# A streaming encoder step: 44 of 48 merge-gate blocks by Strassen's seven products

## The chip, the cores and the metric

One core of one Trainium2 chip runs the kernel in one launch. The metric is the device time of that core in microseconds, smaller is better; an execution is timed from outside, and one further execution is profiled instruction by instruction.

## The reference, cut to what matters

One layer for 640 tokens (512 of a prompt, 8 streams of 16): a pre-norm, one projection to the heads of three attention branches and to three merge gates of the model width, the attentions, and the merge. The change concerns the gates.

```python
D_MODEL = 2048
x2 = rms_norm(x, g_pre)                      # 640 tokens
mg_sb, mg_bd, mg_mm = split(x2 @ w_in)[-3:]  # 3 gates of 2048 columns each
merged = (sigmoid(mg_sb) * ((o_sb * silu(g_sb)) @ w_up_sb)
          + sigmoid(mg_bd) * ((o_bd * silu(g_bd)) @ w_up_band)
          + sigmoid(mg_mm) * ((o_mm * silu(g_mm)) @ w_up_mem))
y = x + rms_norm(merged @ w_out, g_post)
```

## The kernel before, in words

All operands are float32, and every matmul is done as three float32r matmuls. `split` (line 91) cuts an operand into a high part, which ACT writes (line 92), and the residual, which DVE computes (line 93); the products high by high, high by low and low by high are added up in PSUM. Transposed x stands in SBUF as `xh` and `xl` (128 partitions, 16 blocks of the model width, 640 tokens).

A projection block, `proj` (line 129), yields 128 output columns for all 640 tokens. It loads the block's weights in slabs of 8 x 128 rows (`load_w`, line 95: `wr` has three buffers, `wh` and `wl` two each), splits them, and for each of 16 k issues three matmuls for each half of 320 tokens (line 139), 96 in all, into two PSUM banks. The program order is: the prologue (pre-norm by `norm_x`, memory keys and values); 16 heads, each with four projections and its attention, its gated output `sg` written to DRAM (`spill`, line 516); then the merge; then the output projection.

The merge runs over 48 gate blocks (`gate`, line 587) and 48 up-projection blocks (`up`, line 601), 16 of each for each of the three branches. `up(i)` follows four blocks behind `gate(i)`, the sigmoid of a gate stays in SBUF in between. At the first block of a branch `up` loads the branch's heads back from DRAM (`load_o`, line 593: `or` has two buffers, `oh` and `ol` six) and splits them. DVE multiplies the block by its sigmoid (lines 611, 613), and from the second branch on POOL adds it to `merged` (line 614).

```python
for i in range(3 * KB + AHEAD):
    if i < 3 * KB:
        gate(i)
    if i >= AHEAD:
        up(i - AHEAD)
gh, gl = xh, xl
```

A scheduler puts the instructions of each engine in order, from this program text and its own model of the engines; it lets later blocks fill the gaps of earlier ones, so the first gate blocks stand between the instructions of the last head. Each engine, and each DMA queue, then works strictly in its order. A pool of tiles that is opened after another was closed reuses its space, and the first instruction that writes a tile there waits for the last ones that used what lies under it.

Of the kernel before, what the change touches and what calls it, by code (L numbers as in the profile page):

```python
# [41 lines left out]
def stream_step_kernel(  # L42
# [19 lines left out]
    xpool = ctx.enter_context(tc.tile_pool(name="xpool", bufs=1, side="right"))  # L62
# [4 lines left out]
    # 1 where a new key of the same stream lies strictly before the query, and the complement;  # L67
    # rows in the order of the sample columns, keys in that of the streams
# [3 lines left out]
    xh = xpool.tile([P, KB, NT], F32R, name="xh")  # L72
    xl = xpool.tile([P, KB, NT], F32R, name="xl")
# [3 lines left out]
    osg_d = [dpool.tile([P, NT], F32, name=f"osg_d{i}") for i in range(16)]  # L77

    # Sample row or column 32 j + 16 a + i is token i of stream 4 a + j.
    def blocks(t_, prompt, sample, t):  # L80
        """Pieces of the token block t and the DRAM rows that go with them."""
        if t < 4:
            return [(t_, prompt[t * P:(t + 1) * P])]
        rows = [32 * (b % 4) + TS * (b // 4) for b in range(NB)]
        return [(t_[r:r + TS], sample[b * TS:(b + 1) * TS]) for b, r in enumerate(rows)]

    def stream_order(ap):
        """A [128, 128] operand with its 128 sample columns in the order of the streams."""
        return ap.rearrange("p (j a i) -> p a j i", a=2, i=TS)

    def split(hi, lo, src):
        ACT.copy(hi, src)  # L92
        DVE.tensor_tensor(lo, src, hi.bitcast(F32), op=ALU.subtract)  # L93

    def load_w(src, shape, pool=None, bufs=None):
        """A 4 KB slab of weights, split into two float32r parts."""
        raw = pw.tile(shape, F32, tag="wr", name="wr", bufs=B["wr"])
        SP.dma_start(raw, src)
        wh = (pool or pw).tile(shape, F32R, tag="wh", name="wh", bufs=bufs or B["wh"])
        wl = (pool or pw).tile(shape, F32R, tag="wl", name="wl", bufs=bufs or B["wl"])  # L100
# [28 lines left out]
    def proj(w, col, kn, src, acc, half=8):  # L129
        """acc[:, s] = w[:, col:col+128]^T @ src^T over kn blocks of 128 rows."""  # L130
        for k0 in range(0, kn, half):
            n = min(half, kn - k0)
            wh, wl = load_w(w[k0 * P:(k0 + n) * P, col:col + P].rearrange("(k p) c -> p k c", p=P), [P, n, P])
            for k in range(n):
                bh, bl = src(k0 + k)
                first, last = k0 + k == 0, k0 + k == kn - 1
                for a, b, f, l in ((wh, bh, True, False), (wh, bl, False, False), (wl, bh, False, True)):
                    for s in range(2):
                        PE.matmul(acc[:, s, :HF], a[:, k], b[:, s * HF:(s + 1) * HF],  # L139
                                  start=first and f, stop=last and l)  # L140

    def x_src(k):
        return xh[:, k], xl[:, k]
# [8 lines left out]
    with ExitStack() as m0:  # L152
# [55 lines left out]
        def norm_x(t):  # L208
# [48 lines left out]
    # operands with fixed zeros: two streams share a group of 32 columns  # L257
# [5 lines left out]
    def masked(t, lead):  # L263
        """The 16-column pieces of a zero-padded operand that hold data, in stream order."""
# [33 lines left out]
    def natural_new(src, outs, name):  # L298
        """The sample columns of a [128, 640] operand by stream, and token-major, which is written out."""
# [9 lines left out]
    def head_k(col, outp, outs):  # L309
# [7 lines left out]
        # 32 x 32 blocks are transposed; the DMA puts them in their places  # L317
# [36 lines left out]
    def causal_prompt(q, k, v, sg, kind, strip):  # L354
        """Stick-breaking or chunk-causal softmax over the prompt, two query blocks at a time."""
# [40 lines left out]
    def stick(b, e, n):  # L396
        """b <- b[s] * prod of e[j] over j > s; the last column of b is 0."""
# [4 lines left out]
    def softmax(p, s, scale=1.0):  # L402
        """p <- softmax(scale * s) along the free axis."""
# [28 lines left out]
    def sample_att(ck, cv, qr, kr, vn, sg, kind, strips):  # L432
# [10 lines left out]
        def load_k(b):  # L443
            """Keys of streams b, b + 1, cut so that transposing 32 x 32 blocks yields K^T."""
# [140 lines left out]
    sigs, parts = {}, {}  # L585

    def gate(i):
        acc = new_acc()
        proj(w_in, C_GATE + i * P, KB, x_src, acc)
        sigs[i] = stg.tile([P, NT], F32, tag="sig", name="sig", bufs=AHEAD + 2)  # L590
        ACT.activation(halves(sigs[i]), acc[:, :, :HF], AF.Sigmoid)
# [8 lines left out]

    def up(i):
# [6 lines left out]
        proj(w_up[0], j * P, nh, lambda k: parts[k], acc)  # L608
        sig = sigs.pop(i)
# [24 lines left out]
    for cb in range(4):  # L634
# [30 lines left out]
        for t in (4, 0, 1, 2, 3):  # L665
            xs = []
            for c in (slice(0, D // 2), slice(D // 2, D)):
# [3 lines left out]
                xs.append(x)  # L671
# [42 lines left out]
```

## Time and profile before

| what | us |
|---|---|
| median of 3 runs | 2257.32 (2255.58 to 2258.13) |
| profiled execution, span from first to last instruction | 2257.1 |
| PE busy | 2212.0 (98%) |
| DVE busy | 796.9 (35%) |
| ACT busy | 607.2 (27%) |
| POOL busy | 190.5 (8%) |

For the profiled execution the profile gives the span and no further time of its own; the span lies within the times of the runs. PE is TensorE, PEld its weight loads, DVE the vector engine, ACT the scalar engine, POOL GpSimd, SP the engine that issues most DMAs. A matmul's busy time is the time it is in flight; several are at once, so the rate is read from the distance of the starts. L139 is line 139 of the kernel before.

### The profile page before, as it was taken

How to read it: one execution, taken by the hardware profiler on the slowest of the kernel's cores; microseconds unless marked ns; L12 is line 12 of the kernel's file. 1: busy time of each engine (PE TensorE's matmuls, PEld its weight loads, DVE VectorE, ACT ScalarE, POOL GpSimd, SP SyncE). 2: the span in 40 equal slices, each digit the busy share in tenths (PEclk: the TensorE clock that was granted, in tenths of full speed). 3: DMA queues.
4: the chain of work that ended last, by engine and by line, in shares of the span. 5: the costliest groups of instructions: out<-in, count | busy, mean ns of one | idle time of the engine just before them, and what ended most of it. 6: DMA issues, size and time to landing. Idle time of an engine off the chain costs nothing.

```text
span 2257.1 us, 34856 instructions
## 1 busy us (share of the span) xinstructions
PE 2212.0 (98%) x14805; PEld 2062.3 (91%) x14805; DVE 796.9 (35%) x1185; ACT 607.2 (27%) x936; POOL 190.5 (8%) x265
## 2 busy tenths in 40 slices
PE   6989999999999999999999999999999999999997
PEld 4888898898989989988999999999999999998886
DVE  7624434444344444444332222231221222252224
ACT  6422333333323233232332111121111221132221
POOL 4100001001000100101000000001111111120000
PEclk9999999999999999999999999999999999999998
DMA  7665456456546646555523222232222222233225
GB/s 234 176 145 112 124 131 149 129 121 151 136 110 158 153 107 152 143 114 135 133 88 95 77 78 77 69 112 78 71 75 78 85 71 80 80 96 115 75 77 166
DMA packets 605225, 257.01 MB, mean 114 GB/s; under 512 B 275952, under 2 KB 581120, under 8 KB 604044
## 3 DMA queue, kind: packets, MB, share of 16 engines
q1 hardware_dynamic: 598892, 237.45, 40.6%
q0 software_dynamic: 3872, 13.13, 1.7%
q10 hardware_dynamic: 2304, 4.20, 0.5%
q8 instruction: 116, 1.90, 0.4%
q14 instruction: 41, 0.34, 0.1%
HBM read 234.25 MB, written 20.46 MB: 113 GB/s over the span
## 4 chain that ended last, share of the span: by engine, by line
PE 94%; DVE 2%; DMA 1%; issue 1%; SPq 1%; ACT 1%; ACTq 0%; POOL 0%; DVEq 0%; POOLq 0%
PE acc L139 74%; PE s L462 3%; PE ya L126 3%; PE ya L127 3%; PE ya L125 3%; PE o L507 1%; DMA st<-rext_d 1%; DVE wl L93 1%; PE tp L385 1%; PE s L125 1%; PE o L126 1%; PE acc L126 1%; PE acc L127 0%; PE tp L219 0%; PE acc L125 0%
## 5 line engine op out<-in xcount | busy, mean ns | idle before, releaser
L139 PE MATMUL acc<-xh,wl 128*128 128x320 f32 x3328 | 771.6, 311 | 0.0
L139 PE MATMUL acc<-xl,wh 128*128 128x320 f32 x3328 | 771.1, 311 | 0.0
L139 PE MATMUL acc<-xh,wh 128*128 128x320 f32 x3328 | 768.2, 311 | 0.0
L93 DVE TENSOR_TENSOR wl<-wr,wh 128x1024 fp32r<-128x1024 f32 (+2 forms) x304 | 368.2, 1212 | 894.9 <-ACT wh L92 874.9
L92 ACT CAST wh<-wr 128x1024 fp32r<-128x1024 f32 (+2 forms) x304 | 305.0, 1004 | 1106.5 <-PE acc L139 832.1
L139 PEld LDWEIGHTS acc<-xh,wh 128*128 128x128 f32 x3328 | 558.3, 188 | 23.8 <-issue 22.6
L139 PEld LDWEIGHTS acc<-xh,wl 128*128 128x128 f32 x3328 | 559.4, 188 | 18.0 <-issue 17.5
L139 PEld LDWEIGHTS acc<-xl,wh 128*128 128x128 f32 x3328 | 559.1, 188 | 11.8 <-issue 11.6
L614 POOL TENSOR_TENSOR merged<-merged,sig 128x640 f32<-128x640 f32 x32 | 77.2, 2412 | 775.1 <-DVE sig L613 775.1
L126 PE MATMUL ya<-wl,xh 128*128 128x512 f32 x320 | 126.8, 396 | 0.4 <-DVE wl L93 0.4
L127 PE MATMUL ya<-wh,xl 128*128 128x512 f32 x320 | 126.6, 396 | 0.0
L125 PE MATMUL ya<-wh,xh 128*128 128x512 f32 x320 | 125.7, 396 | 0.0
L139 PE MATMUL acc<-oh,wh 128*128 128x320 f32 x512 | 116.8, 309 | 0.0
L139 PE MATMUL acc<-ol,wh 128*128 128x320 f32 x512 | 116.8, 309 | 0.0
L139 PE MATMUL acc<-oh,wl 128*128 128x320 f32 x512 | 116.8, 309 | 0.0
L458 DVE STREAM_TRANSPOSE kt<-kc 128x512 f32<-128x512 f32 (+1 forms) x128 | 75.0, 622 | 89.4 <-PE s L462 48.5
L139 PEld LDWEIGHTS acc<-ol,wh 128*128 128x128 f32 x512 | 85.5, 188 | 0.0
L139 PEld LDWEIGHTS acc<-oh,wh 128*128 128x128 f32 x512 | 85.5, 188 | 0.0
L139 PEld LDWEIGHTS acc<-oh,wl 128*128 128x128 f32 x512 | 85.5, 188 | 0.0
L462 PE MATMUL s<-kt,qm 128*32 128x512 f32 (+1 forms) x256 | 83.8, 551 | 0.0
L126 PEld LDWEIGHTS ya<-wl,xh 128*128 128x128 f32 x320 | 60.3, 189 | 15.1 <-DVE wl L93 0.8
L127 PEld LDWEIGHTS ya<-wh,xl 128*128 128x128 f32 x320 | 60.3, 189 | 14.3
(171 smaller groups left out, 1450.6 us busy)
## 6 DMA issues: line engine op xcount, KB each, us to landing
wr<-in_w_in_dram SPq DMA_DIRECT2D x208, 512.0 KB, 3.8
wr<-in_w_out_dram SPq DMA_DIRECT2D x32, 512.0 KB, 3.9
kc<-in_cache_sb_k_dram SPq DMA_DIRECT2D x96, 128.0 KB, 3.7
vc<-in_cache_sb_v_dram SPq DMA_DIRECT2D x48, 256.0 KB, 4.9
kc<-in_cache_band_k_dram SPq DMA_DIRECT2D x96, 128.0 KB, 3.4
vc<-in_cache_band_v_dram SPq DMA_DIRECT2D x48, 256.0 KB, 5.1
wr<-in_w_mem_kv_dram SPq DMA_DIRECT2D x16, 512.0 KB, 4.8
wr<-in_w_up_sb_dram SPq DMA_DIRECT2D x16, 384.0 KB, 3.3
```

The lines of the kernel that those rows point to most:

```text
L92: ACT.copy(hi, src)
L93: DVE.tensor_tensor(lo, src, hi.bitcast(F32), op=ALU.subtract)
L125: PE.matmul(out, ah, bh, start=start, stop=False)
L126: PE.matmul(out, ah, bl, start=False, stop=False)
L127: PE.matmul(out, al, bh, start=False, stop=stop)
L139: PE.matmul(acc[:, s, :HF], a[:, k], b[:, s * HF:(s + 1) * HF], start=first and f, stop=last and l)
L385: PE.transpose(tp[:, kb * P:(kb + 1) * P], b[:, kb * P:(kb + 1) * P], ident)
L458: DVE.transpose(kt[:, :nc_], kc[:, h * nc_:(h + 1) * nc_])
L462: PE.matmul(s[32 * j:32 * j + 32, :nc_], qm[:, j, par * 32:par * 32 + 32], kts[j][:, :nc_], start=par == 0, stop=par == 1, tile_position=( ...
L507: PE.matmul(o[32 * j:32 * j + 32, :P], l, r, start=i == 0, stop=i == len(steps) - 1, tile_position=(0, 32 * j))
L614: POOL.tensor_tensor(merged[:, j], merged[:, j], sig, op=ALU.add)
```

## The change

The first four gate blocks are computed as before, each sigmoid then written to DRAM (`put_sig`). The other 44 are taken in pairs. For a pair the product of a 256 x 2048 piece of transposed weights with the 2048 x 640 transposed x is cut in 2 x 2 blocks: a11 to a22 (128 columns, 8 blocks of 128 rows each) and b11 to b22 (the tiles of x by 8 k and 320 tokens). `gate_pair` forms the four outputs with seven products of 24 matmuls instead of eight. The sums of x that the scheme needs (t1, t2, t4, and t3 in place of b12) are made once, by `sums` and `sums_last` in 8 rounds each; the sums of weights (s1 to s4) by POOL for each pair (`comb`). All 48 up-projections follow after the last gate, with `gh` and `gl` in tiles of their own on the space of x, and read the sigmoids back from DRAM. The rest of the diff takes comments out and renames.

```diff
-AHEAD = 4
+FIRST = 4
-    xh = xpool.tile([P, KB, NT], F32R, name="xh")
-    xl = xpool.tile([P, KB, NT], F32R, name="xl")
+    xq = [[tuple(xpool.tile([P, KH, HF], F32R, name=f"x{n}{i}{j}") for n in "hl") for j in range(2)] for i in range(2)]
+    sig_d = [dpool.tile([P, NT], F32, name=f"sig_d{i}") for i in range(3 * KB)]
...
-                split(xh[:, kg * 4:kg * 4 + 4, t * P:(t + 1) * P],
-                      xl[:, kg * 4:kg * 4 + 4, t * P:(t + 1) * P], tp.rearrange("p (i n) -> p i n", i=4))
+                tv = tp.rearrange("p (i n) -> p i n", i=4)
+                for j in range(2):
+                    a, b = max(t * P, j * HF), min((t + 1) * P, (j + 1) * HF)
+                    if a < b:
+                        h, l = (xq[kg // 2][j][n][:, kg % 2 * 4:kg % 2 * 4 + 4, a - j * HF:b - j * HF] for n in range(2))
+                        split(h, l, tv[:, :, a - t * P:b - t * P])
...
+    tpool = gs.enter_context(tc.tile_pool(name="tpool", bufs=1, reuse_waits="tile"))
+    tt = ts.enter_context(tc.tile_pool(name="tt", bufs=1, reuse_waits="tile"))
+    def put_sig(i, sig):
+        ACT.dma_start(sig_d[i], sig)
...
+    b11, b12, b21, b22 = xq[0][0], xq[0][1], xq[1][0], xq[1][1]
+    t1, t2, t4 = (tuple(tpool.tile([P, KH, HF], F32R, name=f"t{n}{i}") for n in "hl") for i in (1, 2, 4))
+    t3 = b12
+    def whole(eng, q, k, name):
+        t = tt.tile([P, HF], F32, tag=name, name=name)
+        eng.tensor_tensor(t, q[0][:, k].bitcast(F32), q[1][:, k].bitcast(F32), op=ALU.add)
+        return t
+    def sums(k):
+        r = [whole(POOL if n % 2 else DVE, q, k, f"r{n}") for n, q in enumerate((b11, b12, b21, b22))]
+        for t, a, b in ((t1, r[1], r[0]), (t2, r[3], r[0]), (t4, r[2], r[0])):
+            DVE.tensor_tensor(r[0], a, b, op=ALU.subtract)
+            split(t[0][:, k], t[1][:, k], r[0])
+    def sums_last(k):
+        r1, r3 = (whole(POOL, q, k, f"r{n}") for n, q in ((1, b12), (3, b22)))
+        DVE.tensor_tensor(r1, r3, r1, op=ALU.subtract)
+        split(t3[0][:, k], t3[1][:, k], r1)
+    for i in range(FIRST):
+        gate(i)
+        for k in range(i * KH // FIRST, (i + 1) * KH // FIRST):
+            sums(k)
+    for k in range(KH):
+        sums_last(k)
+    ts.close()
+    sw = gs.enter_context(tc.tile_pool(name="sw", bufs=1, reuse_waits="tile"))
+    def load_quads(col):
+        raws = []
+        for h in range(2):
+            for c in range(2):
+                pool, n = ((pw, "wr"), (sw, "wr2"))[c]
+                t = pool.tile([P, 4, 2 * P], F32, tag=n, name=n, bufs=B["wr"])
+                r = (h * KH + c * 4) * P
+                SP.dma_start(t, w_in[r:r + 4 * P, col:col + 2 * P].rearrange("(k p) c -> p k c", p=P))
...
+        def comb(eng, a, b, op):
+            t = sw.tile([P, KH, P], F32, tag="ws", name="ws", bufs=3)
+            for c, o in enumerate(pieces(t)):
+                eng.tensor_tensor(o, a[c], b[c], op=op)
+            return pieces(t)
+        def product(bank_, w, x, first):
+            wh = pw.tile([P, KH, P], F32R, tag="wh", name="wh", bufs=B["wh"])
+            wl = pw.tile([P, KH, P], F32R, tag="wl", name="wl", bufs=B["wl"])
+            for c in range(2):
+                split(wh[:, 4 * c:4 * c + 4], wl[:, 4 * c:4 * c + 4], w[c])
+            for k in range(KH):
+                for n, (a, b) in enumerate(((wh, x[0]), (wh, x[1]), (wl, x[0]))):
+                    PE.matmul(bank_, a[:, k], b[:, k], start=first and k == 0 and n == 0, stop=k == KH - 1 and n == 2,
+                              skip_group_check=not first)
...
+        qa, qb = half(), half()
+        product(qa, a11, b11, True)
+        p1 = keep(qa, "p1")
+        s1 = comb(POOL, a21, a22, ALU.add)
+        s2 = comb(POOL, s1, a11, ALU.subtract)
+        product(qb, a12, b21, True)
+        DVE.tensor_tensor(o0[:, lo], p1, qb, op=ALU.add)
+        product(qa, s2, t2, False)
+        u2 = keep(qa, "u2")
+        qc = half()
+        product(qc, s1, t1, True)
+        p5 = keep(qc, "p5")
+        s3 = comb(POOL, a11, a21, ALU.subtract)
+        product(qa, s3, t3, False)
+        DVE.tensor_tensor(o1[:, hi], p5, qa, op=ALU.add)
+        s4 = comb(POOL, a12, s2, ALU.subtract)
+        product(qc, s4, b22, False)
+        DVE.tensor_tensor(o0[:, hi], u2, qc, op=ALU.add)
+        ACT.activation(o0, o0, AF.Sigmoid)
+        put_sig(i, o0)
+        product(qa, a22, t4, False)
...
+    for i in range(FIRST, 3 * KB, 2):
+        gate_pair(i)
...
+        sig = po.tile([P, NT], F32, tag="sig", name="sig")
+        SP.dma_start(sig, sig_d[i])
...
-    for i in range(3 * KB + AHEAD):
-        if i < 3 * KB:
-            gate(i)
-        if i >= AHEAD:
-            up(i - AHEAD)
-    gh, gl = xh, xl
+    for i in range(3 * KB):
+        up(i)
+    gh, gl = (gpool.tile([P, KB, NT], F32R, name=n) for n in ("gh", "gl"))
```

The scheduler's order changes with it. On DVE, after the last work of the last head (`sg`, the gated output), there stood residuals of gate weights (`wl`) and of the heads for the up-projections (`ol`):

```order
L495 COPY wn_11119<-t2_11117 128x128
L93 TENSOR_TENSOR wl_11619<-wr_11616,wh_11618 128x1024
L514 TENSOR_TENSOR sg_10564<-t3_11159,sg_10564 128x128
L93 TENSOR_TENSOR wl_11673<-wr_11670,wh_11672 128x1024
L93 TENSOR_TENSOR ol_11729<-or_11726,oh_11728 128x640
L93 TENSOR_TENSOR ol_11735<-or_11732,oh_11734 128x640
```

Now a round of `sums` follows at once (r0 to r3 are the sums of high and low parts, th and tl the split results; line numbers are those of the changed kernel):

```order
L522 TENSOR_TENSOR sg_10626<-t3_11221,sg_10626 128x128
L612 TENSOR_TENSOR r0_11350<-xh00_73,xl00_74 128x320
L612 TENSOR_TENSOR r2_11354<-xh10_77,xl10_78 128x320
L619 TENSOR_TENSOR r0_11350<-r1_11352,r0_11350 128x320
L96 TENSOR_TENSOR tl1_11233<-r0_11350,th1_11232 128x320
L619 TENSOR_TENSOR r0_11350<-r3_11356,r0_11350 128x320
L96 TENSOR_TENSOR wl_11933<-wr_11886,wh_11932 128x512
L96 TENSOR_TENSOR tl2_11235<-r0_11350,th2_11234 128x320
L619 TENSOR_TENSOR r0_11350<-r2_11354,r0_11350 128x320
L612 TENSOR_TENSOR r2_11371<-xh10_77,xl10_78 128x320
L96 TENSOR_TENSOR tl4_11237<-r0_11350,th4_11236 128x320
```

Seven more rounds of this kind and the eight of `sums_last` stand before the next residual of weights; the first of them, for the second half of the first pair's first product, comes right behind the last sum:

```order
L625 TENSOR_TENSOR r1_11864<-r3_11866,r1_11864 128x320
L96 TENSOR_TENSOR xl01_76<-r1_11864,xh01_75 128x320
L625 TENSOR_TENSOR r1_11871<-r3_11873,r1_11871 128x320
L96 TENSOR_TENSOR xl01_76<-r1_11871,xh01_75 128x320
L96 TENSOR_TENSOR wl_11895<-wr2_11884,wh_11894 128x512
L96 TENSOR_TENSOR wl_11933<-wr2_11888,wh_11932 128x512
L96 TENSOR_TENSOR wl_11964<-ws_11929,wh_11963 128x512 x2
L687 TENSOR_TENSOR sig_11890<-p1_11924,q_11893 128x320
```

Nothing else in the program moved on DVE ahead of this place but the splits of x. The tile `wr2_11884`, read here, is the first of its pool, and its load on SP waits for the residual `xl01_76<-r1_11871` above it.

## Rows read from the trace of the kernel before

**Rows 1.** The page, its part 1: busy us (share of the span) and instructions.
```profile
PE 2212.0 (98%) x14805; PEld 2062.3 (91%) x14805; DVE 796.9 (35%) x1185; ACT 607.2 (27%) x936; POOL 190.5 (8%) x265
```
**Rows 2.** The page, part 4: the chain that ended last, by engine and line.
```profile
PE 94%; DVE 2%; DMA 1%; issue 1%; SPq 1%; ACT 1%; ACTq 0%; POOL 0%; DVEq 0%; POOLq 0%
PE acc L139 74%; PE s L462 3%; PE ya L126 3%; PE ya L127 3%; PE ya L125 3%; PE o L507 1%; DMA st<-rext_d 1%; DVE wl L93 1%; PE tp L385 1%; PE s L125 1%; PE o L126 1%; PE acc L126 1%; PE acc L127 0%; PE tp L219 0%; PE acc L125 0%
```
**Rows 3.** Window: us; PE, PEld, DVE, ACT, POOL busy; PE clock, DMA share, GB/s.
```profile
1200.00:1300.00 100.00, 100.00 (x684) 100.00 (x683) 21.98 (x21) 17.91 (x21) 0.00 (x0) 1.00 0.26 74
```
**Rows 4.** Timeline around the last head: start us, us, engine, line, operation, count.
```profile
1166.80 0.27 PE L513 MATMUL t<-ident,on 128*128 128x128 f32 x1
...
1167.20 0.46 PE L139 MATMUL acc<-xl,wh 128*128 128x320 f32 x2
...
1167.49 0.46 PE L139 MATMUL acc<-xh,wl 128*128 128x320 f32 x2
```
**Rows 5.** The same timeline, DVE and POOL.
```profile
1168.09 0.28 DVE L514 TENSOR_TENSOR sg<-t,sg 128x128 f32<-128x128 f32 x1
...
1168.67 0.54 POOL L517 DMA_DIRECT2D osg_d<-sg  x1 [38.91 <-DVE sg L514]
```
**Rows 6.** DMA issues from 1165 to 1185: count, KB each, median us to landing.
```profile
osg_d<-sg POOLq DMA_DIRECT2D x1, 320.0 KB, 6.0
```
**Rows 7.** Line 93, DVE, by form; line 92, ACT (ns min/median/max).
```profile
L93 DVE TENSOR_TENSOR kl<-kr,kh 128x512 fp32r<-128x512 f32 x12 | 8.0, 664 | 3.1 <-ACT kh L92 3.1
...
L93 DVE TENSOR_TENSOR ql<-acc,qh 128x320 fp32r<-128x320 f32 x16 | 7.7, 482 | 0.0
...
L92 ACT CAST kh<-kr x12: 620/624/632, 156.2 to 1102.8; 128x512 fp32r<-128x512 f32 x12
L92 ACT CAST vh<-vnm x4: 405/405/405, 283.2 to 826.3; 128x256 fp32r<-128x256 f32 x4
```
**Rows 8.** Timeline, a softmax that goes from DVE to ACT and back.
```profile
1151.26 0.82 DVE L405 TENSOR_REDUCE sm<-b 128x1 f32<-128x640 f32 x1
...
1151.99 0.42 DVE L393 TENSOR_TENSOR sg<-o,sg 128x256 f32<-128x256 f32 x1
...
1152.11 0.83 ACT L408 ACTIVATE b<-b,sm 128x640 f32<-128x640 f32 x1 [3.07 <-DVE sm L405]
...
1152.85 0.19 ACT L408 ACTIVATION_READ_ACCUMULATOR b<-b,sm 128x1 f32 x1
...
1153.07 0.17 DVE L409 RECIPROCAL sm<-sm 128x1 f32<-128x1 f32 x1 [0.66 <-ACT b L408]
...
1153.27 0.55 DVE L410 TENSOR_SCALAR b<-b,sm 128x640 f32<-128x640 f32 x1
```
**Rows 9.** Timeline, DVE beside POOL additions and products.
```profile
23.43 4.61 POOL L213 TENSOR_TENSOR xr<-xr,gbx 128x2048 f32<-128x2048 f32 x1 [20.50 <-ACT junk L161]
23.60 4.46 DVE L114 TENSOR_TENSOR rsm<-rsm 128x1 f32<-128x1 f32 x1
...
2008.47 2.02 POOL L614 TENSOR_TENSOR merged<-merged,sig 128x640 f32<-128x640 f32 x1 [1.63 <-DVE sig L613]
...
2008.97 2.07 DVE L93 TENSOR_TENSOR wl<-wr,wh 128x512 fp32r<-128x512 f32 x1
```
**Rows 10.** DMA issues of the page; us to landing of `or`.
```profile
wr<-in_w_in_dram SPq DMA_DIRECT2D x208, 512.0 KB, 3.8
...
DMA to landing us min/median/max: 2.8/4.3/6.2
```
**Rows 11.** A wait of PE; windows after it (columns as rows 3).
```profile
163.49 0.47 PE L304 MATMUL t<-ident,knT 128*128 128x128 f32 x1 [4.49 <-POOL knT L301]
...
160.00:165.00 5.00, 1.51 (x6) 1.41 (x7) 0.00 (x0) 0.27 (x1) 1.35 (x4) 0.83 1.05 283
165.00:170.00 5.00, 5.00 (x29) 4.86 (x29) 1.47 (x2) 2.02 (x3) 0.71 (x3) 0.82 0.51 103
```
**Rows 12.** Windows, the prologue.
```profile
40.00:60.00 20.00, 14.14 (x68) 10.98 (x66) 19.22 (x17) 13.01 (x17) 14.87 (x3) 0.99 0.71 151
```

More of the change, by code (lines that the diff above doesn't have):

```diff
@@ L19 @@
 KB = D // P
+KH = KB // 2
 TP = 512
@@ L61, in stream_step_kernel @@
     const = ctx.enter_context(tc.tile_pool(name="const", bufs=1))
-    xpool = ctx.enter_context(tc.tile_pool(name="xpool", bufs=1, side="right"))
+    xs = ExitStack()
+    xpool = xs.enter_context(tc.tile_pool(name="xpool", bufs=1, side="right"))
     dpool = ctx.enter_context(tc.tile_pool(name="dpool", bufs=1, space=DRAM))
@@ L138, in proj @@
                     for s in range(2):
-                        PE.matmul(acc[:, s, :HF], a[:, k], b[:, s * HF:(s + 1) * HF],
+                        PE.matmul(acc[:, s, :HF], a[:, k], b[s],
                                   start=first and f, stop=last and l)
     def x_src(k):
-        return xh[:, k], xl[:, k]
+        h, l = ([xq[k // KH][j][n][:, k % KH] for j in range(2)] for n in range(2))
+        return h, l
     def new_acc():
@@ L578, in stream_step_kernel, with gate @@
     att.close()
+    gs = ExitStack()
+    tpool = gs.enter_context(tc.tile_pool(name="tpool", bufs=1, reuse_waits="tile"))
+    ts = ExitStack()
+    tt = ts.enter_context(tc.tile_pool(name="tt", bufs=1, reuse_waits="tile"))
+    def put_sig(i, sig):
+        ACT.dma_start(sig_d[i], sig)
+    def gate(i):
+        acc = new_acc()
+        proj(w_in, C_GATE + i * P, KB, x_src, acc)
+        sig = stg.tile([P, NT], F32, tag="sig", name="sig")
+        ACT.activation(halves(sig), acc[:, :, :HF], AF.Sigmoid)
+        put_sig(i, sig)
@@ new lines, in sums_last @@
+    def sums_last(k):
[18 more added lines that the diff above has]
+                SP.dma_start(t, w_in[r:r + 4 * P, col:col + 2 * P].rearrange("(k p) c -> p k c", p=P))
+                raws.append(t)
+        return [[[raws[2 * h + c][:, :, b * P:(b + 1) * P] for c in range(2)] for h in range(2)] for b in range(2)]
@@ new lines, in pieces, with gate_pair, half, keep @@
+    def pieces(t):
+        return [t[:, 4 * c:4 * c + 4] for c in range(2)]
+    def gate_pair(i):
+        (a11, a12), (a21, a22) = load_quads(C_GATE + i * P)
+        def comb(eng, a, b, op):
[12 more added lines that the diff above has]
+                              skip_group_check=not first)
+        def half():
+            return bank("q")[:, :HF]
+        def keep(src, name):
+            t = sw.tile([P, HF], F32, tag=name, name=name)
+            ACT.copy(t, src)
+            return t
+        o0, o1 = (stg.tile([P, NT], F32, tag="sig", name="sig") for _ in range(2))
+        lo, hi = slice(0, HF), slice(HF, NT)
+        qa, qb = half(), half()
[19 more added lines that the diff above has]
+        product(qa, a22, t4, False)
+        ACT.activation(o1[:, hi], o1[:, hi], AF.Sigmoid)
+        ACT.activation(o1[:, lo], qa, AF.Sigmoid)
+        put_sig(i + 1, o1)
@@ L581, in stream_step_kernel @@
+    for i in range(FIRST, 3 * KB, 2):
+        gate_pair(i)
+    gs.close()
+    xs.close()
+    gpool = ctx.enter_context(tc.tile_pool(name="gpool", bufs=1, side="right", reuse_waits="tile"))
     pm = br.enter_context(tc.tile_pool(name="mraw", bufs=1, reuse_waits="tile"))
@@ L584, in stream_step_kernel @@
     branches = ((w_up_sb, 6, 0), (w_up_band, 6, 6), (w_up_mem, 4, 12))
[L585 to L591, printed above, removed]
+    parts = {}
     def load_o(i):
@@ L599, in load_o, with o_src @@
         return hh, ll
+    def o_src(k):
+        return [[t[:, j * HF:(j + 1) * HF] for j in range(2)] for t in parts[k]]
     def up(i):
@@ L606, in up @@
                 parts[h] = load_o(i0 + h)
+        sig = po.tile([P, NT], F32, tag="sig", name="sig")
+        SP.dma_start(sig, sig_d[i])
         acc = new_acc()
-        proj(w_up[0], j * P, nh, lambda k: parts[k], acc)
-        sig = sigs.pop(i)
+        proj(w_up[0], j * P, nh, o_src, acc)
         if i < KB:
@@ L665, in stream_step_kernel @@
         for t in (4, 0, 1, 2, 3):
-            xs = []
+            xres = []
             for c in (slice(0, D // 2), slice(D // 2, D)):
@@ L670, in stream_step_kernel @@
                     SP.dma_start(v, src)
-                xs.append(x)
+                xres.append(x)
             for sl in slabs:
@@ L680, in stream_step_kernel @@
                 c = slice(q * 512, (q + 1) * 512)
-                DVE.scalar_tensor_tensor(yt[t][:, c], yt[t][:, c], r, xs[q // 2][:, q % 2 * 512:q % 2 * 512 + 512],
+                DVE.scalar_tensor_tensor(yt[t][:, c], yt[t][:, c], r, xres[q // 2][:, q % 2 * 512:q % 2 * 512 + 512],
                                          op0=ALU.mult, op1=ALU.add)
```

## The prediction

> **What bounds the kernel now.** I read the busy shares first: TensorE works 98% of the span [rows 1]. The chain that ended last says the same from the end: 94% of it is PE, and the matmuls of line 139, the projections, are 74% [rows 2]. Then one stretch in the middle of the gates: in 100 us PE starts 684 matmuls and is never idle, at a granted clock of 1.00 (2.4 GHz), while the vector engine (DVE) works 22 us, the scalar engine (ACT) 18, GpSimd (POOL) none, and the DMA engines a quarter [rows 3]. So in the gates a matmul left out is time won, as long as the other engines keep up; and whatever makes PE wait outside the gates is added in full. The price of a matmul is its pitch, not the 311 ns that it is in flight: two start every 0.293 us [rows 4], 0.1465 us each.
>
> **What is removed.** A gate block is 16 x 3 x 2 = 96 matmuls of 320 columns; 44 blocks are 4224. A pair now has 7 products of 8 x 3 = 24, and 22 pairs have 3696. 528 fewer at 0.1465 us is **-77.4 us**, all of it on PE. The Trainium skill (TensorE: Matmul & The Clock Gate, Back-to-back issue gap) gives N / 2.4 + 2.5 ns for an isolated matmul, by which 320 columns would take 136 ns and the saving would be an estimated 72 us; the rows have 0.1465 us, and they decide.
>
> **What is added, and where PE waits for it.** Up to the last matmul of gate 3 the PE order is that of before, so the clock times of the trace hold. The last transpose of the last head starts at 1166.80 [rows 4]; 42 matmuls of gate 3 follow, to 1173.0. The order then has 24 matmuls (the first halves of products 1 and 2) whose raw weights come from the old pool: done at 1176.5. Everything after needs a tile `wr2`. Its buffer lies over r0 to r3, and its load waits for the last subtraction of `sums_last`. So all 16 rounds of sums lie between, and they can't start early: they stand in the DVE and POOL queues behind the last head's work (1168.09 on DVE, [rows 5]), and the first cast of `sums` waits until the last head's o * gate has landed in DRAM, since t1 takes over the space of that tile: issued 1168.67 [rows 5], 6.0 us to landing [rows 6], so 1174.7.
>
> A round of `sums` is a serial chain, since its three differences go through the one tile r0. A DVE operation of 320 columns took 0.48 us, an ACT cast between 0.41 (256) and 0.62 (512 columns), so 0.46 [rows 7]; an engine answers another after 0.03 us and itself, when it needs its own result, after 0.03, which I set to 0.04 [rows 8]. Cast, hop, residual, gap, difference, hop is 1.52 us; three of these and one sum of 0.52 make 5.08. POOL's two sums of the round come on top in part: while POOL multiplied a 128x2048 tile for 4.61 us, a DVE product of one column took 4.46 (a reciprocal of one column takes 0.17); and a 512-column residual that takes 0.66 took 2.07 beside a POOL addition of 640 columns [rows 7 to 9]. The two took turns, and POOL needs 4.61 / 2048 = 2.25 ns a column, 0.72 us for 320. Most of that falls into DVE's waits for ACT; about 0.25 us each does not. So 5.6 us a round: seven rounds 39.2, plus 0.7 for a cast and a residual of weights that stand in the first. The eighth overlaps the first rounds of `sums_last`: 7.0 to the second difference there. A further round of that loop is POOL r3, then the delayed residual, POOL r1, the difference: 2.7 us, six of them 16.2. The last cast and residual take 1.0, and POOL's first combinations, which nothing holds back, cut in for 1.8. The end is 1174.7 + 0.7 + 39.2 + 7.0 + 16.2 + 1.0 + 1.8 = 1240.6. A 512 KB weight load lands 3.8 us after issue [rows 10], its first half is cast in 0.62 [rows 7]: PE goes on at 1245, after **68.4 us** of idling from 1176.5. Bounds: with no hold by POOL at all the chain is 7.6 us shorter; if every POOL addition costs its recorded 2.02 us per 640 columns and more (waits included, 6.4 and 3.5 us a round), 11.5 us longer. I take the middle value, since rows 9 show turns, and no more.
>
> On resuming, the residual of the first half stands behind a POOL combination (512 columns, 1.15 us): 1.0 us. After an idle stretch of 4.49 us PE's granted clock was 0.83 and 0.82 in the two next 5 us windows [rows 11]; that is about 2 us at half speed lost. **+3**, between 1 and 5.
>
> The 22 pairs: a product takes 24 x 0.1465 = 3.52 us. Its weight tiles are free when the last but one product ends, and are split in 0.62 + 2 x 0.66 = 1.9 us [rows 7]; the second half is only needed 1.76 us into the product. The copies, additions and sigmoids stand in the queues behind the next product's split, by the order. POOL's eight combinations are 9.2 us of a pair's 24.6, DVE's operations 14 x 0.66 + 3 x 0.48 = 10.7: 20 us together even if they never overlap. The three PSUM halves are each read one product before they are added to again. I set **+1.5** for all pairs, between 0 and 22 (1 us a pair).
>
> The up-projections lose their cover. Before, loading and splitting the heads lay under gate matmuls; now PE has nothing else. At the start `or` (two buffers) loads three times in turn. A load takes 4.3 us (2.8 to 6.2, [rows 10]), cast and residual of 640 columns about 1.55, so the sixth head is ready about 17.7 us after the last product and PE ends blocks 0 and 1 at 18.9, where their 72 matmuls need 10.6: 8.4 us lost, 1.1 more for the next weights, which wait for these tiles, 0.5 for the clock: **+10**, between 6 and 17. At the two changes of branch two heads are loaded ahead: **+2.5**, between 0 and 6. The sigmoids' way through DRAM is hidden: written on ACT's queue, read five blocks ahead; DMA rises from 74 GB/s at a share of 0.26 [rows 3] to some 110 with the pairs.
>
> The prologue: DVE is busy 19.2 of 20 us there [rows 12], and four splits become eight smaller ones: **+1**, between 0 and 1.5.
>
> Sum: -77.4 + 68.4 + 3 + 1.5 + 10 + 2.5 + 1 = +9.0. The profiled execution spans 2257.1 us, 0.2 below the median of the runs (2257.32), so I make no correction: 2266.1, **2266**. A change below 0.2% (4.5 us) can't be told from none.
>
> **Rivals.** (a) Faster: the sums run at the pace of DVE's work, not as a chain. For it: independent DVE operations start some 0.09 us before the one ahead has ended in the record (1151.99 after 1151.26 + 0.82, [rows 8]); 64 + 16 operations at 0.41 are 33 us. The chain would end at about 1211, PE idle 41 us, the total 2239. It decides below an idle stretch of 59 us. Against it: every operation there waits on its forerunner, which costs the whole duration and 0.04 us. (b) The gate stage becomes bound by the turns of DVE and POOL: if a residual waits for a combination of 1.15 us twice per product and the lag adds up, 1 to 3 us a pair, 22 to 66 in all; 2288 and more, 2300 where it is mild. For it speaks the 4.46 us of rows 9. Against it: 20 of 24.6 us. The Trainium skill (SBUF — State Buffer, Who interferes with whom) says that a DVE instruction with two SBUF inputs and a GpSimd instruction that reads SBUF exclude each other for the whole instruction; rows 9 agree with it, 4.46 us against 0.17. (c) The sums are as short as without POOL's hold and the up-projections start at their lower bound: -77.4 + 60.8 + 3 + 1.5 + 6 + 2.5 + 1 = -2.6, no change, 2255.
>
> **How the numbers follow.** The forecast gets 0.56, (a) 0.14, (b) 0.12, (c) 0.18. The forecast's own range is 2255 to 2282; 2250 to 2290 also takes in (c) and the mild end of (b), and leaves out most of (a) and half of (b). Faster: (a) and a little of (c), 0.16; same: the rest of (c) and the forecast's lower edge, 0.18; slower: 0.66.
>
> **What would show it.** In the new trace: PE idle from about 1177 to about 1245, ended by a cast of `wh` from `wr2`, with the residual of the last sum some 4 us before; sums rounds of 5 to 6 us; pairs of 24.6 us; another gap of some 10 us, in pieces, at the first up-projection. The prediction is wrong if that first gap is below 59 us, or a pair takes over 25.5 us.

## The result and the profile after

The changed kernel takes 2267.79 us (median of 4 runs, 2267.2 to 2268.0), the kernel before 2257.73 (4 runs, 2255.58 to 2258.18): ratio 1.0044, 95% interval 1.003 to 1.0058. It is slower, by 10 us; 2266 was forecast. The profiled execution spans 2266.1 us. The page's first part for it:

```profile
PE 2146.3 (95%) x14277; PEld 1991.9 (88%) x14277; DVE 1063.2 (47%) x1555; ACT 730.5 (32%) x1280; POOL 485.9 (21%) x473
```

Against [rows 1] PE has 528 matmuls fewer and is busy 66 us less, but now only 95% of the span. In the chain that ended last PE had 94% [rows 2]; now:

```profile
PE 82%; DVE 6%; issue 4%; DMA 3%; POOL 2%; ACT 1%; SPq 1%; ACTq 0%; DVEq 0%; POOLq 0%
```

DVE, POOL and the loads have entered it. The waits of PE behind the last head show where the rest went (waited for: us in total, times, longest):

```profile
PE q L668 <- ACT wh L95: 66.0, 1, 66.0
PE acc L142 <- ACT oh L95: 9.0, 4, 4.8
```

The others are of 1.0 us in total or less. One wait of 66.0 us holds most of it. The windows over that stretch (columns as in [rows 3]) show which engines work in it:

```profile
1170.00:1190.00 20.00, 4.45 (x31) 4.19 (x29) 14.34 (x26) 5.69 (x12) 6.02 (x7) 0.73 0.05 18
1190.00:1210.00 20.00, 0.00 (x0) 0.00 (x0) 15.71 (x30) 4.58 (x10) 5.15 (x6) 0.50 0.00 0
1210.00:1230.00 20.00, 0.00 (x0) 0.00 (x0) 10.87 (x18) 4.07 (x9) 12.04 (x14) 0.50 0.00 0
1230.00:1250.00 20.00, 9.18 (x41) 8.78 (x42) 9.33 (x11) 4.76 (x9) 10.55 (x10) 0.57 0.41 131
```

From 1190 to 1230 PE starts no matmul, the DMA engines move nothing, and none of DVE, ACT and POOL is busy all the time either: the mark of a chain that goes from engine to engine. One round of `sums` in the timeline (start us, us, engine, line, operation, idle before and releaser):

```profile
1174.94 0.49 DVE L619 TENSOR_TENSOR r<-r,r 128x320 f32<-128x320 f32 x1
1175.47 0.46 ACT L95 CAST th<-r 128x320 fp32r<-128x320 f32 x1 [1.68 <-DVE r L619]
1175.52 0.86 POOL L612 TENSOR_TENSOR r<-xh,xl 128x320 f32<-128x320 f32 x1 [4.63 <-DVE r L619]
1175.96 0.76 DVE L96 TENSOR_TENSOR tl<-r,th 128x320 fp32r<-128x320 f32 x1 [0.52 <-ACT th L95]
1176.83 0.49 DVE L619 TENSOR_TENSOR r<-r,r 128x320 f32<-128x320 f32 x1
...
1177.84 0.76 DVE L96 TENSOR_TENSOR tl<-r,th 128x320 fp32r<-128x320 f32 x1 [0.52 <-ACT th L95]
1178.64 0.49 DVE L619 TENSOR_TENSOR r<-r,r 128x320 f32<-128x320 f32 x1
1179.16 0.49 DVE L612 TENSOR_TENSOR r<-xh,xl 128x320 f32<-128x320 f32 x1
1179.16 0.46 ACT L95 CAST th<-r 128x320 fp32r<-128x320 f32 x1 [1.35 <-DVE r L619]
1179.65 0.49 DVE L96 TENSOR_TENSOR tl<-r,th 128x320 fp32r<-128x320 f32 x1
1180.18 0.49 DVE L612 TENSOR_TENSOR r<-xh,xl 128x320 f32<-128x320 f32 x1
1180.77 0.49 DVE L619 TENSOR_TENSOR r<-r,r 128x320 f32<-128x320 f32 x1
```

Difference, cast, residual, three times, from 1174.94 to 1180.77: 5.83 us a round. Two of the three residuals take 0.76 us instead of 0.49; beside these POOL adds. The end of the chain:

```profile
1235.17 0.95 DVE L96 TENSOR_TENSOR xl<-r,xh 128x320 fp32r<-128x320 f32 x1 [0.52 <-ACT xh L95]
...
1236.18 2.02 SPq L645 DMA_DIRECT2D wr<-in_w_in_dram  x4
1239.81 0.62 ACT L95 CAST wh<-wr 128x512 fp32r<-128x512 f32 x1 [4.67 <-DMA wr<-in_w_in_dram]
...
1240.46 1.21 DVE L96 TENSOR_TENSOR wl<-wr,wh 128x512 fp32r<-128x512 f32 x1 [4.34 <-ACT wh L95]
1240.48 0.64 PE L668 MATMUL q<-xh,wh 128*128 128x320 f32 x1 [66.03 <-ACT wh L95]
```

The last residual ends at 1236.12, the load of `wr2` goes out at 1236.18 and its cast begins at 1239.81. From 1241.72 on the pairs run without a gap; a window in them, beside which [rows 3] stands, and the piece of the chain of waits (start, us, what) that covers them all:

```profile
1300.00:1400.00 100.00, 100.00 (x684) 100.00 (x683) 57.54 (x69) 42.25 (x82) 52.27 (x34) 1.00 0.34 111
```
```profile
1241.72 541.07 PE q L668 x3670
```

3670 matmuls at the pitch of 0.1465 us are 537.7 us, so 22 pairs and the slow matmuls at their beginning cost 3.4 us together.

### The profile page after: what moved, and what is told of

Read it like the earlier page. It is cut to its first block, busy times and chain, and to the rows that moved or that the text cites. A ratio compares the mean times of both kernels' runs of the same rounds, so it can differ in the third digit from the quotient of the medians.

```text
span 2266.1 us, 35309 instructions
## 1 busy us (share of the span) xinstructions
PE 2146.3 (95%) x14277; PEld 1991.9 (88%) x14277; DVE 1063.2 (47%) x1555; ACT 730.5 (32%) x1280; POOL 485.9 (21%) x473
## 4 chain that ended last, share of the span: by engine, by line
PE 82%; DVE 6%; issue 4%; DMA 3%; POOL 2%; ACT 1%; SPq 1%; ACTq 0%; DVEq 0%; POOLq 0%
PE acc L142 39%; PE q L668 24%; PE s L470 3%; PE ya L129 3%; PE ya L130 3%; PE ya L128 3%; DVE wl L96 2%; POOL merged L744 2%; PE o L515 1%; DMA sig<-sig_d 1%; DMA wr<-in_w_in_dram 1%; DVE tl L96 1%; PE tp L393 1%; PE o L129 1%; PE s L128 1%
## 5 line engine op out<-in xcount | busy, mean ns | idle before, releaser
L142 PE MATMUL acc<-xh,wl 128*128 128x320 f32 x1920 | 450.2, 312 | 0.0
L142 PE MATMUL acc<-xl,wh 128*128 128x320 f32 x1920 | 449.9, 312 | 0.0
L142 PE MATMUL acc<-xh,wh 128*128 128x320 f32 x1920 | 447.0, 312 | 0.0
L142 PEld LDWEIGHTS acc<-xh,wh 128*128 128x128 f32 x1920 | 322.4, 188 | 23.7 <-issue 22.6
L142 PEld LDWEIGHTS acc<-xh,wl 128*128 128x128 f32 x1920 | 323.6, 188 | 18.0 <-issue 17.5
L142 PEld LDWEIGHTS acc<-xl,wh 128*128 128x128 f32 x1920 | 323.2, 188 | 11.8 <-issue 11.6
L668 PE MATMUL q<-xh,wh 128*128 128x320 f32 x704 | 219.0, 311 | 66.0 <-ACT wh L95 66.0
L96 DVE TENSOR_TENSOR wl<-ws,wh 128x512 fp32r<-128x512 f32 x176 | 170.0, 1005 | 119.3 <-ACT wh L95 119.1
L668 PE MATMUL q<-xh,wl 128*128 128x320 f32 x704 | 218.8, 311 | 0.3 <-DVE wl L96 0.3
L668 PE MATMUL q<-xl,wh 128*128 128x320 f32 x704 | 218.7, 311 | 0.0
```

The lines of the kernel that those rows point to most:

```text
L142: PE.matmul(acc[:, s, :HF], a[:, k], b[s], start=first and f, stop=last and l)
L668: PE.matmul(bank_, a[:, k], b[:, k], start=first and k == 0 and n == 0, stop=k == KH - 1 and n == 2, skip_group_check=not first)
```

## Experiments

Each kernel is the changed kernel with the edit shown; the kernel before ran beside it (medians 2257.63 to 2257.83).

**e1: a tile of its own for each difference, two sets.**

```diff
-        t = tt.tile([P, HF], F32, tag=name, name=name)
+        t = tt.tile([P, HF], F32, tag=name, name=name, bufs=2)
-            DVE.tensor_tensor(r[0], a, b, op=ALU.subtract)
-            split(t[0][:, k], t[1][:, k], r[0])
+            d = tt.tile([P, HF], F32, tag="d", name="d", bufs=6)
+            DVE.tensor_tensor(d, a, b, op=ALU.subtract)
+            split(t[0][:, k], t[1][:, k], d)
```

(and likewise in `sums_last`). It takes each difference against the first sum; in the changed kernel the second and third start from the difference before. So t2 and t4 are not the sums that the scheme needs, and this kernel serves for its time alone; one with tiles of its own and the right operands was not run. The operations and their sizes are the same.

> Each difference goes to a tile of its own, and all tiles of the sums come twice. Theory (the sums are a serial chain through r0 and r1, 5.83 us a round of sums and 2.75 us a round of sums_last in the changed kernel's trace): without the chain DVE sets the pace, 8 operations of 0.49 us and some waiting for POOL, 4.5 us a round, and POOL's two additions of 0.86 us set it in sums_last, 1.8 us a round. The idle stretch of PE shrinks from 66.0 to some 48 us, the time from 2267.8 to about 2250. Rival (DVE and POOL exclude each other for whole operations, and that sets the pace): 8 x 0.49 + 2 x 0.7 = 5.3 us a round and 2.7 for the last ones; idle 61 us, time about 2263.

Measured: 2251.97 us (2250.43 to 2253.2), ratio 0.9975 (0.9965 to 0.9984); the wait is 47.0 us. So the chain was the cause of 19 of the 66 us; the other 47 are left without it, at the pace of DVE and POOL. That pace was not the one expected throughout: POOL stood behind DVE. Its timeline where DVE's queue was full:

```profile
1189.06 6.67 POOL L612 TENSOR_TENSOR r<-xh,xl 128x320 f32<-128x320 f32 x1 [4.05 <-DVE d L620]
```
```profile
1188.50 2.49 DVE L620 TENSOR_TENSOR d<-r,r 128x320 f32<-128x320 f32 x6
1190.91 0.48 DVE L96 TENSOR_TENSOR tl<-d,th 128x320 fp32r<-128x320 f32 x1
1191.31 0.88 DVE L612 TENSOR_TENSOR r<-xh,xl 128x320 f32<-128x320 f32 x2
1192.12 1.28 DVE L96 TENSOR_TENSOR tl<-d,th 128x320 fp32r<-128x320 f32 x3
1193.32 0.88 DVE L612 TENSOR_TENSOR r<-xh,xl 128x320 f32<-128x320 f32 x2
1194.13 0.88 DVE L96 TENSOR_TENSOR tl<-d,th 128x320 fp32r<-128x320 f32 x2
```

An addition that takes 0.86 us in the changed kernel lasts 6.67 us, to 1195.73, while DVE runs without a pause until 1195.01. The Trainium skill (SBUF — State Buffer, Who interferes with whom) says that a DVE instruction with two SBUF inputs and a GpSimd instruction that reads SBUF exclude each other and that the one which comes second waits for the first. The residuals of 0.76 us agree: POOL's addition ends at 1176.38, the residual 0.34 us later. This row goes further than the page: fourteen DVE instructions start and end within POOL's addition, not one, and it ends 0.72 us after the last of them, the time that the prediction works out for 320 columns on POOL.

**e2: the first pair's loads free of the sums.**

```diff
+    sw = gs.enter_context(tc.tile_pool(name="sw", bufs=1, reuse_waits="tile"))
     ts = ExitStack()
     tt = ts.enter_context(tc.tile_pool(name="tt", bufs=1, reuse_waits="tile"))
...
     ts.close()
-    sw = gs.enter_context(tc.tile_pool(name="sw", bufs=1, reuse_waits="tile"))
+    sv = gs.enter_context(tc.tile_pool(name="sv", bufs=1, reuse_waits="tile"))
...
-        s3 = comb(POOL, a11, a21, ALU.subtract)
+        s3 = comb(POOL, a11, a21, ALU.subtract, True)
```

`comb` takes its tile for s3 from the late pool `sv`; s1, s2 and s4 share two tiles of `sw`.

> wr2, p1, u2, p5 and two of the three tiles of weight sums get space that the tiles of the sums do not use, so the first pair's loads no longer wait for the last sum. The sums stay as they are. Theory (the space of wr2 is why PE stands still before the second half of product 1): products 1 to 4 of the first pair (96 matmuls, of which 24 were done before the stretch) run beside the sums, and only product 5, which needs t3, waits for the last round, to about 1240. 72 matmuls of 0.1465 us are then done earlier: about 10 us gained, time about 2258, the long idle stretch of PE in two pieces or more. Rival (the order of DVE, not the space, holds PE: the sums stand in the queue anyhow): no change, 2268.

Measured: 2261.15 us (2258.7 to 2263.02), ratio 1.0013 (1.0004 to 1.0023). PE's waits from 1170 to 1260:

```profile
PE q L669 <- ACT wh L95: 22.1, 1, 22.1
PE q L669 <- ACT th L95: 17.1, 12, 4.7
PE q L669 <- DVE tl L96: 3.1, 13, 1.1
PE q L669 <- DVE wl L96: 2.5, 1, 2.5
```

The wait fell apart as expected: product 3 follows the sums round by round (waits for `th` and `tl`), and only 22.1 us for `sums_last` are left. The space of `wr2` and its pool was what held all 66 us in one piece. The gain is 6.6 us, not 10: the residuals of products 1 to 4 now stand among the sums, whose last residual ends at 1242.85 (1236.12 in the changed kernel), so PE goes on with product 5 at 1244.90 instead of the expected 1240.

**e3: eight gate blocks first** (`FIRST = 8`).

> Eight gate blocks instead of four are computed as before, and 20 pairs instead of 22 follow. Theory (the 66 us are work of DVE, ACT and POOL that has no matmuls beside it): gates 4 to 7 take 56 us of PE and lie beside the eight rounds of sums, stretched to about 7 us each by the residuals of gate weights in DVE's queue; then the 22 us of sums_last and the load are left. PE's longest wait falls from 66 to about 22 us; two pairs fewer leave out 24 matmuls less each, 7 us. Time about 2267.8 - 44 + 7 = 2231. Rival (the residuals of gate weights behind links of the chain hold PE up as well): idle over 40 us in pieces, time 2250 or more.

Measured: 2230.46 us (2228.92 to 2231.82), ratio 0.9879 (0.9864 to 0.9894). PE waits 20.2 us there in place of 66.0:

```profile
PE q L668 <- ACT wh L95: 20.2, 1, 20.2
```

So the sums are work that lacked matmuls beside it: four more gates hide 46 of 66 us of it, at the price of 48 matmuls, 7 us.

**e4: the heads for the up-projections early.**

```diff
-    pm = br.enter_context(tc.tile_pool(name="mraw", bufs=1, reuse_waits="tile"))
     po = br.enter_context(tc.tile_pool(name="osgp", bufs=6, reuse_waits="tile"))
+    pm = br.enter_context(tc.tile_pool(name="mraw", bufs=1, reuse_waits="tile"))
...
-        r = po.tile([P, NT], F32, tag="or", name="or", bufs=2)
-        SP.dma_start(r, osg_d[i])
+        r = po.tile([P, NT], F32, tag="or", name="or", bufs=6)
+        POOL.dma_start(r, osg_d[i])
...
-        sig = po.tile([P, NT], F32, tag="sig", name="sig")
+        sig = po.tile([P, NT], F32, tag="sig", name="sig", bufs=2)
```

> The heads for the up-projections get the space of t1 and t2, which are read for the last time in products 3 and 4 of a pair, and six tiles for the loads; the loads go out on POOL's queue. Theory (the first up-projection starts late because the loads wait for the last product, and then two at a time): PE's first wait there falls from 4.85 to about 2.3 us (the casts stand behind the last sigmoid), the second of 2.57 and most of the low clock after them vanish, the branch changes lose about 1 us: some 9 us gained, time about 2259. Rival (weights and casts set the start, not the loads of the heads): no more than 2 us, time 2266.

Measured: 2257.87 us (2254.78 to 2260.1), ratio 1.0 (0.999 to 1.0009): 9.9 us less than the changed kernel. Of the four waits for `oh` this one is left, and the wait of 66 us is as it was:

```profile
PE q L668 <- ACT wh L95: 66.1, 1, 66.1
PE acc L142 <- ACT oh L95: 2.3, 1, 2.3
```

**e5_all: the edits of e2, e3 and e4 together**, and the last sums in two sets of tiles in turn:

```diff
-        r1, r3 = (whole(POOL, q, k, f"r{n}") for n, q in ((1, b12), (3, b22)))
+        r1, r3 = (whole(POOL, q, k, f"r{n - k % 2}") for n, q in ((1, b12), (3, b22)))
```

> Three edits together: eight gate blocks ahead of the pairs, the first pair's loads and first products on space of their own, the heads for the up-projections early; and the last sums use r1, r3 and r0, r2 in turn, so that a round need not wait for the one before. Theory (the standing still of PE is placement, not work): sums end at about 1225 beside gates 4 to 7, the last sums 18 to 24 us later, beside products 1 to 4; PE's idle time there falls to some 6 us. 2267.8 - 66 - 3.5 (clock) + 6 + 7 (two pairs fewer) - 10 (heads) = 2201. Rival (the products of the first pair wait behind sums in DVE's queue): idle 20 us and a low clock, 2217 or more.

Measured: 2211.36 us (2209.74 to 2213.14), ratio 0.9792 (0.9776 to 0.9808). It is 10 us above what was expected, between theory and rival. The windows show it (columns as in [rows 3]):

```profile
1230.00:1240.00 10.00, 6.75 (x30) 6.09 (x30) 8.59 (x11) 4.21 (x9) 8.54 (x10) 0.72 0.08 33
1240.00:1250.00 10.00, 9.24 (x58) 8.72 (x56) 8.01 (x11) 2.82 (x7) 6.71 (x7) 0.94 0.00 0
1250.00:1260.00 10.00, 5.08 (x24) 4.96 (x25) 3.88 (x6) 2.96 (x6) 5.93 (x6) 0.83 0.35 105
1260.00:1270.00 10.00, 9.28 (x63) 9.02 (x62) 6.57 (x8) 4.76 (x9) 5.80 (x5) 1.00 0.36 102
```

From 1230 to 1270 PE starts 169 matmuls, counted in the timeline, where a full PE starts 273: 104 times 0.1465 us are 15.2. (A window counts a matmul that crosses its border too, so the sums of the counts above are higher; 107 and 15.7 in the expectation of e7_mixed below come from them.) Only 9.7 us are waits (2.4, 0.8, 0.8, 4.9, 0.7); the rest goes to matmuls at the low clock after them (0.72, 0.94 and 0.83 in the windows), which the expectation had left out.

**e5_first6: the same with six gate blocks.**

> As the kernel with all edits, with six gate blocks ahead of the pairs instead of eight. Theory: gates 4 and 5 cover 28 us, products 1 and 2 another 7; the sums end at about 1222, so product 3 waits some 14 us and product 5 some 9 for the last sums. One pair more is worth 3.5 us. 2267.8 - 66 - 3.5 + 23 + 2 (clock) + 3.5 - 10 = 2217, so eight beats six by some 16 us. Rival (the last sums hide better beside products 3 and 4 than beside a gate): within 4 us of the other.

Measured: 2229.51 us (2227.85 to 2230.35), ratio 0.9874 (0.9859 to 0.9889). Eight beat six by 18 us, as the theory had it; they lie 10 and 13 us above its figures.

**e6: all sums on DVE.**

```diff
-        r = [whole(POOL if n % 2 else DVE, q, k, f"r{n}") for n, q in enumerate((b11, b12, b21, b22))]
+        r = [whole(DVE, q, k, f"r{n}") for n, q in enumerate((b11, b12, b21, b22))]
-        r1, r3 = (whole(POOL, q, k, f"r{n}") for n, q in ((1, b12), (3, b22)))
+        r1, r3 = (whole(DVE, q, k, f"r{n}") for n, q in ((1, b12), (3, b22)))
```

> The changed kernel with the sums of high and low parts all on DVE, none on POOL. Theory (an addition on POOL holds up the DVE operation beside it, 0.76 us instead of 0.49 in the trace, and the chain waits for POOL): a round of sums falls from 5.83 to about 5.15 us, since DVE's additions fit into the waits for ACT's casts, one of sums_last from 2.75 to about 2.1; PE's wait from 66 to about 55 us, time about 2257. Rival (POOL's additions lie beside the chain and cost nothing; more work on DVE makes it longer): 2268 or more.

Measured: 2258.23 us (2257.03 to 2260.79), ratio 1.0006 (0.9996 to 1.0015); the wait is 56.3 us. A round of its timeline, by the first and the last of the differences:

```profile
1180.47 0.49 DVE L619 TENSOR_TENSOR r<-r,r 128x320 f32<-128x320 f32 x1
...
1185.62 0.49 DVE L619 TENSOR_TENSOR r<-r,r 128x320 f32<-128x320 f32 x1
```

5.15 us a round, as expected to the hundredth, with 16 additions more on DVE from `sums` alone. Help from POOL made the chain longer.

**c_changed_again and c_before_again: controls.** No edit.

> The changed kernel once more, as a control: 2268, with a wait of PE of 66 us. The start of that wait was 1174.45 in its first profile, and what comes ahead of it is the same program but for the splits of x. Theory (the 3 us by which it came earlier than forecast are scatter of the first 170 us, where PE waits for loads): the wait starts elsewhere this time, by 1 us or more, within 1172 to 1179. Rival (the eight smaller splits made the start shorter): 1174 to 1175 again.

> The kernel before once more, as a control for the stretch ahead of the change. The last product of the last head with its gate (DVE, line 514) started at 1168.09 in its first profile, the same instruction of the changed kernel at 1164.8 in one and 1164.6 in another. Theory (the splits of x in eight pieces make the start shorter by 3 us): 1167 to 1169 again. Rival (scatter of the loads at the start): elsewhere, 1163 to 1166.

Measured: 2266.85 us (2265.59 to 2267.65) for the changed kernel, and the wait, again 66.0 us, starts at 1174.23: the rival's case. Then the kernel before (one run, 2256.16 us): the last product of the last head with its gate starts at 1165.4, where [rows 5] had 1168.09. That is the rival's case again, but this rival is scatter, and the first was not.

The product on DVE is not a clean mark. In the kernel before it stood behind a weight residual of 1.23 us that began at 1166.95; in the changed kernel the residual there is one of 0.69 us for the first pair, so 1.0 of the 3.3 us is a change of DVE's order ahead of the sums, which the section on the change does not name. The last head's last transpose on PE tells more. Where [rows 4] have 1166.80, the second profile of the kernel before and the first of the changed one have:

```profile
1164.07 0.27 PE L513 MATMUL t<-ident,on 128*128 128x128 f32 x1
1164.50 0.27 PE L521 MATMUL t<-ident,on 128*128 128x128 f32 x1
```

So one kernel scatters by 2.7 us ahead of the change. The control of the changed kernel has 1164.28, and the same instruction came at 1162.44 (e4) to 1167.41 (e3) in the other profiles. The splits' cost or gain is not resolved; the other 2.3 us lie within the scatter.

**e7_mixed, e5_first10, e7_mixed10: the last sums shared between DVE and POOL, and ten gate blocks first.**

```diff
-        r1, r3 = (whole(POOL, q, k, f"r{n - k % 2}") for n, q in ((1, b12), (3, b22)))
+        r1, r3 = (whole(e, q, k, f"r{n - k % 2}") for e, n, q in ((DVE, 1, b12), (POOL, 3, b22)))
```

> As the kernel with all edits (eight gate blocks first), with one of the two additions of a last sum on DVE, the other on POOL. Measured for that kernel: 2211 us, with 107 matmuls (15.7 us) fewer than a full PE between 1230 and 1270. Theory (there the last sums wait for POOL, whose two additions of a round last 2 us and more beside DVE's work): half of POOL's additions gone, 3 to 6 us are won back, time about 2207. Rival (DVE, which must also make the residuals of products 1 to 4, is the bound there): no change, 2211 or more.

> As the kernel with all edits, with ten gate blocks ahead of the pairs. Theory: the two further gates give the sums 28 us more beside matmuls, but the last sums may only start when the tenth gate has read b12, in the middle of that gate; so 7 us of gate and 14 of products 1 to 4 cover them, and 16 us of eight last sums fit. Of the 15.7 us lost with eight gates all but 3 are won, 3.5 are paid for one pair fewer. 2211 - 12.7 + 3.5 = 2202. Rival (the last sums are held up by their own queue, not by the sums before them): same loss as with eight, 2215.

> Ten gate blocks first and the additions of the last sums shared between DVE and POOL. Theory: 2 us better than with ten gates and POOL alone, 2200, since the last sums end earlier. Rival (with ten gates nothing waits for the last sums any more): the same as with ten gates.

Measured: 2209.05 us (2207.9 to 2211.32; ratio 0.978, 0.9764 to 0.9796) with eight gates and shared additions; 2199.78 (2197.97 to 2201.96; 0.9741, 0.9726 to 0.9756) with ten gates, near the 2202 of the theory and not the 2215 of its rival; 2198.44 (2196.94 to 2199.63; **0.9734, 0.972 to 0.9749**) with both. Sharing seems worth 2.3 us with eight gates, less than the 3 to 6 expected, but the runs of the two kernels overlap (2207.9 to 2211.32 against 2209.74 to 2213.14), so theory and rival are not decided; with ten it is worth no more than the runs scatter. The windows of the last kernel:

```profile
1165.00:1235.00 70.00, 70.00 (x480) 70.00 (x479) 52.07 (x76) 23.01 (x39) 24.69 (x19) 1.00 0.41 127
1235.00:1300.00 65.00, 65.00 (x446) 65.00 (x445) 43.58 (x55) 25.63 (x50) 36.00 (x24) 1.00 0.27 86
```

PE is busy throughout: 16 rounds of sums are made, and nobody waits for them. With 19 pairs, 456 matmuls or 66.8 us are left out; 59.4 of it are won. This version beats both kernels.

## Why the prediction was right, and where it was not

The time (2267.8 for 2266) and the sign came out by the mechanism that was forecast. From the last head's last transpose on PE to the first matmul of the output projection the kernel before takes 851.1 us (2017.86 - 1166.80; 851.1 in the control), the changed one 862.3 (2026.83 - 1164.50; 861.3 in its control): 10.2 to 11.3 more, where the steps made 8.0 for that stretch. Step by step:

| step | forecast | measured |
|---|---|---|
| 528 matmuls fewer | -77.4 | -77.4: 528 fewer, a window of 100 us counts 684 as before |
| PE's wait for the sums | 68.4 (1176.5 to 1245) | 66.0 (1174.45 to 1240.48) |
| resuming and 22 pairs | 3 + 1.5 | 4.2 (2.7 in the control) |
| up-projections | 10 + 2.5 | 19.2 (19.6 in the control) |
| prologue | 1 | not resolved, scatter of 2.7 |

The measured steps add up to 12.0. They count what is lost against a pitch of 0.1465 us, and the kernel before loses 1.1 us against it as well (its 5802 matmuls there need 850.0 us), so they stand for 10.9.

**Matmuls.** The pitch was the price: 528 x 0.1465. Windows in the pairs hold as many matmuls as windows in the gates before. (Of the 684 that the prediction reads as starts, 682 start in the window; the others cross its border.)

**The sums.** That `wr2` lies over the sums' tiles and that a round is a chain through one tile were right: e2 splits the wait by space alone, e1 and e6 shorten the chain. A round took 5.83 us for 5.6, one of the last 2.75 for 2.7. POOL's hold was set at 0.25 us an addition; the residuals show 0.27, and taking POOL out (e6) shortened the wait by 9.7 us, more than the 7.6 of the lower bound: a round fell to 5.15, one of the last to 2.07, and DVE's own additions then lie in its waits for ACT. Wrong was the start: the chain was to wait until the spill had landed, 6.0 us after its issue [rows 6]. It landed in 2.5 us, and the first cast began at 1168.11, 2.7 us after the issue at 1165.40; the profile names the first difference, not the landing, as what it waited for last:

```profile
osg_d<-sg POOLq DMA_DIRECT2D x1, 320.0 KB, 2.5
1168.11 0.46 ACT L95 CAST th<-r 128x320 fp32r<-128x320 f32 x1 [3.97 <-DVE r L619]
```

Counted from the last transpose, the chain began 4.3 us sooner than forecast. Against that stood a first round that took 8 us from difference to difference (1166.88 to 1174.94), with a gate's residual and a sigmoid in it: the chain was 2.1 us longer than forecast, and half of the error was cancelled.

**Resuming and the pairs.** PE waited 0.34 us for the first residual and then ran at the low clock: its matmuls start 0.27 us apart at 1242 to 1247, at a granted clock of 0.50 (1.2 GHz) in the window from 1240 to 1245, 0.76 in the next and 1.00 after that. From 1240.48 to the last product's end, 1782.62 (the start of its last matmul and one pitch), 3672 matmuls took 542.1 us for 537.9. That is 4.2 for both terms, nearly all of it at the start, so a pair loses next to nothing. Rival (b) fell, although DVE's 58 and POOL's 52 us in 100 add up to more than 100: busy times that contain waiting for the other engine overlap (a residual of 512 columns took 0.69 us alone, at 1245.23, and 1.0 on average where it reads a sum of weights).

**The up-projections** were the term mis-sized. From the last product's end to the first matmul of the output projection there are 244.2 us; 1536 matmuls at 0.1465 are 225.0, so 19.2 are lost. By the windows (columns as in [rows 3]):

```profile
1780.00:1790.00 10.00, 5.15 (x28) 4.89 (x28) 3.56 (x4) 3.29 (x6) 0.00 (x0) 0.83 0.82 259
1790.00:1800.00 10.00, 7.43 (x30) 7.14 (x29) 1.65 (x2) 1.45 (x2) 0.00 (x0) 0.67 0.71 248
1800.00:1810.00 10.00, 9.58 (x62) 9.00 (x62) 4.94 (x6) 3.02 (x4) 0.00 (x0) 0.98 0.62 183
```

Between 1782.62 and 1810 the timeline has 98 starts, where a full PE has 187: 13.0 us, of which 4.85 + 2.57 + 0.42 are waits. The granted clock is 0.83 and 0.67 in the first two windows, after the two longer waits; 0.5 us had been set for it. The other 6.2 us lie nearly all at the two changes of branch, for which 0 to 6 was the range: six waits of 0.2 to 0.9 us, 3.5 together, each with the time around it until matmuls start at the full pitch again. e4 won 9.9 of the 19.

So that the time came within 2 us is in part luck: a wait 2.4 us too long and a prologue term of 1 that no run resolves stood against up-projections that were 6.7 too short.

**The other rivals.** (a) needed an idle stretch below 59 us; it was 66.0, and even with tiles of its own for each difference 47.0, not 41. (c) needed POOL's hold to be nothing and the up-projections to start at their lower bound; e6 puts POOL's part in the chain at 9.7 us, and the up-projections lost 13.0 us at their start, not 6.

## What to carry to other kernels

A rearrangement that saves arithmetic needs its preparation placed beside the old arithmetic: here 16 rounds of sums cost 66 us where PE had nothing else, and nothing where ten ordinary blocks stood beside them, at the price of three pairs less. Look where a new tile's space comes from (a load waits for the last reader of what lies under it), and at how many engines a temporary passes before it is free. Giving half of a chain's work to an idle engine can lengthen it, if the two hold each other up.

## What the runs showed of the hardware that was not expected

A POOL addition of 320 columns, 0.86 us beside the chain's pauses, took 6.67 us while DVE worked through additions and subtractions without a pause (e1). The kernel before, profiled twice, reached the same instruction 2.7 us apart after 1165 us, so a term of 1 us can't be read from one profile. After idle stretches of 0.4 to 4.9 us, what was lost beyond the waits came to more than half of them: 5.6 us beside 9.7 us of waits in e5_all (granted clock down to 0.72 in a window of 10 us), 5.2 beside 7.8 at the first up-projections (down to 0.67).
